# Output projection of a hybrid decoder step: the last columns' weights loaded over three column groups, the samples in two halves, two stores a token tile

## The chip, the cores and the metric

The kernel runs on one core of one Trainium2 chip, as one launch. The metric is the device time of that launch in microseconds. A core has five instruction streams that run side by side and wait for one another by semaphores: TensorE (PE in the profile, with PEld for its weight loads), VectorE (DVE), ScalarE (ACT), GpSimd (POOL) and SyncE (SP). Sixteen DMA engines move data; here SP's queue issues the weight loads and the stores of the results, and POOL's queue the loads of the residual rows.

## The reference

One decoder layer (RWKV-7 and HGRN2 branches side by side) on 256 prompt tokens and 64 sample tokens, width 2048, all in float32. The change touches only its last part:

```python
merged = sigmoid(p[..., OFF_GA:OFF_GB]) * (y_a @ proj_a) + sigmoid(p[..., OFF_GB:]) * (y_b @ proj_b)
y = x + merged @ w_out                                   # w_out: 2048 x 2048
y_prompt, y_sample = rms_norm(y, final_norm_g)           # over all 2048 columns of a token
```

The final norm of a token needs the sum of the squares of all its 2048 columns, so no column of a token can be stored before its last column is there.

## The kernel before

The input projection and the two branches (the lines up to 1376, put in order by a planner of the kernel's own) and the merge (lines 1400 to 1420) are not touched. What follows is the output projection with the final norm.

Every float32 operand is held as a high part and a low part (`fp32r`), and a product is made of three matmuls: high times high, low times high, high times low. The 320 tokens are three token tiles, `j` = 0 and 1 for 128 prompt tokens each and `j` = 2 for the 64 samples. For the samples the high and the low part stand side by side as 128 columns of one stationary operand (`ms`), so two matmuls do instead of three, and the two halves of the result's partitions are summed afterwards. The merged tokens are the stationary operand, the weights `w_out` the moving one, 512 columns at a time.

The 2048 columns of `w_out` are four column groups of 512, `n` = 0 to 3; the 2048 rows are 8 steps `kk` of 256 (two `k` of 128 each).

- `columns(n, kk, pool, tag)` (line 1440) loads one piece of 256 x 512 (512 KB): a DMA on SP's queue into `raw`, of which there are three buffers in turn for all pieces; a cast on ACT to `whi`; a subtraction on DVE to `wlo`. With an empty tag `whi` and `wlo` are a ring of three buffers each; with a tag they are tiles of their own in the pool `last`.
- `rows(pt, j, k, hi, lo)` (line 1450) issues the three (or two) matmuls of one `k` for one token tile.
- `add(pt, j, n)` (line 1462) adds the result in PSUM to the residual row in `yx[j]` (for the samples twice, once for each half of the partitions) and squares the 512 columns on ACT, with the sum into one column of `ssq`.

Groups 0 to 2 (from line 1475) run `kk` outermost: each step is 16 matmuls, for the three token tiles in turn, into three PSUM tiles. After a group, `add` is called for each token tile and the columns are multiplied by the gain `fg`. In group 2 each step also calls `columns(3, kk)`, so the last group's eight pieces are loaded beside group 2's own; seven of them have tiles of their own and the eighth takes its place in the ring.

The last columns (from line 1490) run the token tile outermost: all 48 matmuls of tile 0, then its `add`, its norm (`ssq` summed, Ln, Exp, which gives the scale `r`), its four scalings and four stores of 512 columns, while the matmuls of tile 1 run; the same for tile 1; and for the samples 32 matmuls with nothing behind them to cover their norm, scalings and stores.

What sets the order: in groups 0 to 2 PE's instructions stand in the order written, and ACT and DVE are put in order by the framework's scheduler. In the last columns PE, ACT and DVE all stand in the order written. SP issues its DMAs in the order written, each when its buffer is free. The residual rows `yx` and the gains `fg` are loaded by POOL's queue (lines 1429 and 1430) into memory that the input projection held until its last matmul.

Of the kernel before, what the change touches and what calls it, by code (L numbers as in the profile page):

```python
# [9 lines left out]
F32 = mybir.dt.float32  # L10
F32R = mybir.dt.float32r
U8 = mybir.dt.uint8
AF = mybir.ActivationFunctionType
ALU = mybir.AluOpType
# [8 lines left out]
KT = D // 128  # L23
# [249 lines left out]
def hybrid_step(ctx, tc, x_prompt, x_sample, state_rwkv, state_hgrn, state_shift, norm_g, w_in,  # L273
# [3 lines left out]
    nc = tc.nc  # L277
    V, S, G, T = nc.vector, nc.scalar, nc.gpsimd, nc.tensor

    S.add_instruction(mybir.InstLoadActFuncSet(  # L280
        name=nc.get_next_instruction_name(), act_func_set_id=EXP_LN_SET, ins=[], outs=[]))
# [4 lines left out]
    wpool = ctx.enter_context(tc.tile_pool(name="wpool", bufs=1))  # L286
# [67 lines left out]
    with tc.tile_pool(name="start", bufs=1) as st, \  # L354
# [9 lines left out]
        for hf in range(2):  # L364
            cs = slice(1024 * hf, 1024 * hf + 1024)
# [24 lines left out]
        for h in range(2):  # L390
            sl = slice(32 * h, 32 * h + 32)
            G.affine_select(out=sel[sl], in_=sel[sl], pattern=[[-1, 4], [0, 128]],
                            compare_op=ALU.not_equal, fill=1.0, base=0, channel_multiplier=1)
        rows = st.tile([128, 128], F32, name="rows")
        G.memset(rows, 0.0)

        def row_dma(r0, n, src):
# [77 lines left out]
        ssq = [st.tile([128, 2], F32, name=f"ssq{j}") for j in range(3)]  # L475
# [46 lines left out]
        with tc.manual_schedule(engines={mybir.EngineType.PE, mybir.EngineType.Activation, mybir.EngineType.DVE,  # L522
# [70 lines left out]
            for j in range(2):  # L593
                high(j, 3)
                low(j, 3)
            ps = pst.tile([128, 512], F32, name="cps", tag="t")
            T.transpose(ps[:, :128], rows, ident)
            V.tensor_copy(cols, ps[:, :106])
            ps = pst.tile([128, 512], F32, name="sps", tag="t")
# [766 lines left out]
    with tc.manual_schedule():  # L1366
# [3 lines left out]
        V, S, G, T, Y = (book.proxy(e) for e in ("V", "S", "G", "PE", "Y"))  # L1370
        record_all()
        V, S, G, T = real
# [52 lines left out]
    yx = [xa[:, 0], xa[:, 1], xb[:64, 0]]  # L1425
    fg = xb[:, 1]
# [7 lines left out]

    last = ctx.enter_context(tc.tile_pool(name="last", bufs=1))
    pso = ctx.enter_context(tc.tile_pool(name="pso", bufs=2, space=PSUM))
    ssq = last.tile([128, 3, 4], F32, name="ssq")
    rs = [last.tile([128, 1], F32, name=f"rs{j}") for j in range(3)]

    def columns(n, kk, pool, tag):  # L1440
        raw = wpool.tile([128, 2, 512], F32, name="raw", tag="raw", bufs=3)
        nc.sync.dma_start(raw, w_out[0, 256 * kk:256 * kk + 256, 512 * n:512 * n + 512]
                          .rearrange("(k p) c -> p k c", p=128))
        hi = pool.tile([128, 2, 512], F32R, name="whi", tag="whi" + tag, bufs=1 if tag else 3)
        lo = pool.tile([128, 2, 512], F32R, name="wlo", tag="wlo" + tag, bufs=1 if tag else 3)
        S.copy(hi, raw)  # L1446
        V.tensor_sub(lo, raw, hi.bitcast(F32))  # L1447
        return hi, lo

    def rows(pt, j, k, hi, lo):  # L1450
        first, end = k == 0, k == KT - 1
        if j < 2:
            h, l = (t_[:, k, 128 * j:128 * j + 128] for t_ in (mhi, mlo))
            T.matmul(pt, h, hi, start=first, stop=False)  # L1454
            T.matmul(pt, l, hi, start=False, stop=False)  # L1455
            T.matmul(pt, h, lo, start=False, stop=end)  # L1456
        else:
            h = ms[:, k].rearrange("p x t -> p (x t)")
            T.matmul(pt, h, hi, start=first, stop=False)
            T.matmul(pt, h, lo, start=False, stop=end)  # L1460

    def add(pt, j, n):
        y = yx[j][:, 512 * n:512 * n + 512]
        if j < 2:
            V.tensor_add(y, y, pt)
        else:
            for sl in HS:
                V.tensor_add(y, y, pt[sl])
        jk = last.tile([128, 512], F32, name="jk", tag="jk", bufs=2)
        m = y.shape[0]  # L1470
        S.activation(jk[:m], y, AF.Square, accum_out=ssq[:m, j, n:n + 1])

    out_tiles = lambda: [pso.tile([128, 512], F32, name=f"po{j}", tag=f"o{j}") for j in range(3)]
    tail = []
    with tc.manual_schedule(engines={mybir.EngineType.PE}):
        for n in range(3):
            pts = out_tiles()
            for kk in range(8):
                hi, lo = columns(n, kk, wpool, "")
                for q in range(2):  # L1480
                    for j in range(3):
                        rows(pts[j], j, 2 * kk + q, hi[:, q], lo[:, q])
                if n == 2:
                    tail.append(columns(3, kk, *((last, str(kk)) if kk < 7 else (wpool, ""))))
            for j in range(3):
                add(pts[j], j, n)
                y = yx[j][:, 512 * n:512 * n + 512]
                V.tensor_mul(y, y, fg[:y.shape[0], 512 * n:512 * n + 512])

    with tc.manual_schedule(engines={mybir.EngineType.PE, mybir.EngineType.Activation, mybir.EngineType.DVE}):  # L1490
        pts = out_tiles()
        for j in range(3):
            for k in range(KT):
                hi, lo = tail[k // 2]
                rows(pts[j], j, k, hi[:, k % 2], lo[:, k % 2])
            add(pts[j], j, 3)
            m = yx[j].shape[0]
            r = rs[j][:m]
            V.tensor_reduce(r, ssq[:m, j, :], axis=mybir.AxisListType.X, op=ALU.add)
            S.activation(r, r, AF.Ln, scale=1.0 / D, bias=eps_n[:m])  # L1500
            S.activation(r, r, AF.Exp, scale=-0.5)
            dst = y_prompt[0, 128 * j:128 * j + 128, :] if j < 2 else y_sample.rearrange("b l d -> (b l) d")
            for n in (0, 1, 3, 2):
                cs = slice(512 * n, 512 * n + 512)
                y = yx[j][:, cs]
                if n == 0 or n == 2:
                    V.tensor_scalar(y, y, r, 0.0, op0=ALU.mult, op1=ALU.add)
                elif n == 1:
                    S.activation(y, y, AF.Copy, scale=r)
                else:  # L1510
                    V.scalar_tensor_tensor(y, y, r, fg[:m, cs], op0=ALU.mult, op1=ALU.mult)
                nc.sync.dma_start(dst[:, cs], y)


# [26 lines left out]
```

## Time and profile before

| What | us |
|---|---|
| median of three timed runs | 1170.04 (1169.23 to 1171.2) |
| the profiled execution's own time | 1167.92 |
| its span, first to last instruction | 1166.2 |
| first matmul of group 0 | 1035.88 |
| first matmul of group 1, of group 2 | 1064.98, 1094.01 |
| first matmul of the last columns: tile 0, tile 1, samples | 1127.17, 1138.36, 1149.55 |
| last matmul ends | 1157.19 |
| scale of the samples ready | 1160.15 |

All of the trace's times are from the start of the span. In a row of the timeline stand the start and the length in us, the engine, the line, the operation and its operands (out<-in), and in brackets the idle time of the engine before it and what ended that. In a row of a group stand the count, the busy time in us and the mean length of one in ns. In a row of the busy time by stretch stand the stretch and its length, each engine's busy time and number of instructions, the granted clock of TensorE, the busy share of the DMA engines and GB/s. A row of waits has the total in us, the count and the longest.

### The profile page before, as it was taken

The page shows a single profiled execution, that of the slowest core. Times are in us where ns is not written, and L with a number is a line of the kernel's source. Part 1 is how long each engine was busy: PE and PEld are TensorE (multiplying, and loading weights), DVE is VectorE, ACT ScalarE, POOL GpSimd, SP SyncE. Part 2 cuts the span into 40 slices and gives each one's busy share as a digit, 9 for nine tenths or more (in the row PEclk, how much of TensorE's full clock was granted, in tenths as well). Part 3 has the DMA queues.
Part 4 walks back from the last instruction along what each step waited for, and adds up shares of the span by engine and source line. Part 5 has one row for each costly group of instructions (what it writes and reads, how often), then busy time and mean ns, then how long its engine had stood idle before and what let it go on. Part 6 is the DMA issues. An engine that isn't in the chain of part 4 may idle for free.

```text
span 1166.2 us, 20745 instructions
## 1 busy us (share of the span) xinstructions
PE 1140.5 (98%) x7791; PEld 1099.2 (94%) x7791; DVE 779.9 (67%) x1625; ACT 666.7 (57%) x1470; POOL 208.9 (18%) x429
## 2 busy tenths in 40 slices
PE   7899999999999999999999999999999999999996
PEld 6899999999999999999999999999999999988865
DVE  6878878878878778778779786444444444444542
ACT  6666766667667667666676667444444444433431
POOL 8532132222322321321421310000000000000000
PEclk9999999999999999999999999999999999999999
DMA  5734535434435435436335435555555555575532
GB/s 168 197 109 114 146 110 129 138 102 124 136 91 150 128 98 145 127 83 164 102 92 166 123 101 137 149 158 146 147 155 151 145 149 157 146 254 162 180 109 90
DMA packets 283833, 159.69 MB, mean 137 GB/s; under 512 B 22990, under 2 KB 273361, under 8 KB 283093
## 3 DMA queue, kind: packets, MB, share of 16 engines
q1 hardware_dynamic: 283220, 154.70, 47.1%
q0 software_dynamic: 512, 3.67, 1.0%
q8 instruction: 61, 1.00, 0.4%
q14 instruction: 40, 0.32, 0.1%
HBM read 148.53 MB, written 9.81 MB: 136 GB/s over the span
## 4 chain that ended last, share of the span: by engine, by line
PE 92%; DVE 3%; DMA 2%; ACT 1%; POOL 1%; issue 1%; DVEq 0%; SPq 0%; ACTq 0%; POOLq 0%
PE mps L1374 40%; PE a L1374 12%; PE mps L338 6%; PE mps L337 6%; PE mps L339 6%; PE b L1374 4%; DMA raw<-in_w_out_dram 2%; PE po L1456 2%; PE po L1454 2%; PE po L1455 2%; PE ppb L338 2%; PE ppa L338 2%; PE ppb L337 2%; PE ppa L337 2%; PE ppb L339 2%; PE ppa L339 2%
## 5 line engine op out<-in xcount | busy, mean ns | idle before, releaser
L1374 PE MATMUL mps<-hlo,whi 128*128 128x320 f32 x1088 | 344.7, 317 | 0.0
L1374 PE MATMUL mps<-hhi,whi 128*128 128x320 f32 x1088 | 344.1, 316 | 0.0
L1374 PE MATMUL mps<-hhi,wlo 128*128 128x320 f32 x1088 | 343.8, 316 | 0.0
L1374 PEld LDWEIGHTS mps<-hlo,whi 128*128 128x128 f32 x1088 | 204.9, 188 | 4.8 <-issue 4.5
L1374 PEld LDWEIGHTS mps<-hhi,whi 128*128 128x128 f32 x1088 | 204.9, 188 | 1.7 <-issue 1.4
L1374 PEld LDWEIGHTS mps<-hhi,wlo 128*128 128x128 f32 x1088 | 204.9, 188 | 0.2
L328 DVE TENSOR_TENSOR wlo<-raw,whi 128x1024 fp32r<-128x1024 f32 x88 | 107.8, 1225 | 125.3 <-ACT whi L327 125.1
L1374 ACT CAST whi<-raw 128x1024 fp32r<-128x1024 f32 x134 | 140.6, 1049 | 80.3 <-PE mps L1374 75.8
L327 ACT CAST whi<-raw 128x1024 fp32r<-128x1024 f32 x88 | 92.2, 1048 | 163.1 <-PE mps L338 104.8
L1374 DVE TENSOR_TENSOR wlo<-raw,whi 128x1024 fp32r<-128x1024 f32 x134 | 168.1, 1255 | 20.0 <-ACT whi L1374 19.4
L337 PE MATMUL mps<-hhi,whi 128*128 128x320 f32 x448 | 138.4, 309 | 0.0
L338 PE MATMUL mps<-hlo,whi 128*128 128x320 f32 x448 | 138.4, 309 | 0.0
L339 PE MATMUL mps<-hhi,wlo 128*128 128x320 f32 x448 | 138.4, 309 | 0.0
L337 PEld LDWEIGHTS mps<-hhi,whi 128*128 128x128 f32 x448 | 84.1, 188 | 0.0
L338 PEld LDWEIGHTS mps<-hlo,whi 128*128 128x128 f32 x448 | 84.1, 188 | 0.0
L339 PEld LDWEIGHTS mps<-hhi,wlo 128*128 128x128 f32 x448 | 84.1, 188 | 0.0
L1447 DVE TENSOR_TENSOR wlo<-raw,whi 128x1024 fp32r<-128x1024 f32 x32 | 39.0, 1224 | 46.4 <-ACT whi L1446 46.1
L1446 ACT CAST whi<-raw 128x1024 fp32r<-128x1024 f32 x32 | 33.6, 1051 | 56.8 <-DMA raw<-in_w_out_dram 26.9
L1429 POOL DMA_DIRECT2D xb<-in_x_sample_dram x1 | 0.7, 721 | 341.2 <-PE mps L339 341.2
L1454 PE MATMUL po<-whi,mhi 128*128 128x512 f32 x128 | 50.4, 393 | 1.7 <-ACT whi L1446 1.0
L1456 PE MATMUL po<-wlo,mhi 128*128 128x512 f32 x128 | 50.5, 394 | 1.3 <-DVE wlo L1447 1.3
L1455 PE MATMUL po<-whi,mlo 128*128 128x512 f32 x128 | 50.1, 391 | 0.0
(408 smaller groups left out, 2341.4 us busy)
## 6 DMA issues: line engine op xcount, KB each, us to landing
raw<-in_w_in_dram SPq DMA_DIRECT2D x194, 512.0 KB
raw<-in_w_out_dram SPq DMA_DIRECT2D x32, 512.0 KB
raw<-in_proj_a_dram SPq DMA_DIRECT2D x16, 512.0 KB
raw<-in_proj_b_dram SPq DMA_DIRECT2D x16, 512.0 KB
s<-in_state_hgrn_dram SPq DMA_DIRECT2D x8, 512.0 KB
out_dram<-s SPq DMA_DIRECT2D x8, 512.0 KB
s<-in_state_rwkv_dram SPq DMA_DIRECT2D x8, 256.0 KB
out_dram<-s SPq DMA_DIRECT2D x8, 256.0 KB
```

The source lines that it names most:

```text
L327: S.copy(hi[:, ks], raw[:, ks])
L328: sub.tensor_sub(lo[:, ks], raw[:, ks], hi[:, ks].bitcast(F32))
L337: T.matmul(dst, hi[:, q, :], xhi[:, k, :], start=(k == 0), stop=False)
L338: T.matmul(dst, hi[:, q, :], xlo[:, k, :], start=False, stop=False)
L339: T.matmul(dst, lo[:, q, :], xhi[:, k, :], start=False, stop=(k == nk - 1))
L1374: o.fn(*o.args, **o.kw)
L1429: G.dma_start(yx[j], src)
L1446: S.copy(hi, raw)
L1447: V.tensor_sub(lo, raw, hi.bitcast(F32))
L1454: T.matmul(pt, h, hi, start=first, stop=False)
L1455: T.matmul(pt, l, hi, start=False, stop=False)
L1456: T.matmul(pt, h, lo, start=False, stop=end)
```

## The change

The pieces of the last columns are no longer all loaded in group 2. After steps 1, 4 and 7 of each group the next piece is loaded until there are seven: indices 0 to 2 in group 0, 3 to 5 in group 1, 6 in group 2. The eighth is loaded at the head of the last columns.

The samples' last 512 columns are made in two halves of 256: 32 matmuls of 256 columns into one PSUM tile, their `add` into a fourth column of `ssq`, then 32 more into another PSUM tile and their `add` into a fifth.

The scalings of each token tile go to other engines in part (columns 1024 to 1535 from DVE to ACT) and the four stores of 512 columns become two of 1024.

```diff
-    ssq = last.tile([128, 3, 4], F32, name="ssq")
+    ssq = last.tile([128, 3, 5], F32, name="ssq")
...
     def rows(pt, j, k, hi, lo):
+        pt = pt[:, :hi.shape[-1]]
...
-    def add(pt, j, n):
-        y = yx[j][:, 512 * n:512 * n + 512]
+    def add(pt, j, n, c0, w=512):
+        y = yx[j][:, c0:c0 + w]
         if j < 2:
-            V.tensor_add(y, y, pt)
+            V.tensor_add(y, y, pt[:, :w])
         else:
             for sl in HS:
-                V.tensor_add(y, y, pt[sl])
+                V.tensor_add(y, y, pt[sl, :w])
         jk = last.tile([128, 512], F32, name="jk", tag="jk", bufs=2)
         m = y.shape[0]
-        S.activation(jk[:m], y, AF.Square, accum_out=ssq[:m, j, n:n + 1])
+        S.activation(jk[:m, :w], y, AF.Square, accum_out=ssq[:m, j, n:n + 1])
...
-                if n == 2:
-                    tail.append(columns(3, kk, *((last, str(kk)) if kk < 7 else (wpool, ""))))
+                if kk % 3 == 1 and len(tail) < 7:
+                    tail.append(columns(3, len(tail), last, str(len(tail))))
             for j in range(3):
-                add(pts[j], j, n)
+                add(pts[j], j, n, 512 * n)
...
+        tail.append(columns(3, 7, wpool, ""))
         pts = out_tiles()
         for j in range(3):
-            for k in range(KT):
-                hi, lo = tail[k // 2]
-                rows(pts[j], j, k, hi[:, k % 2], lo[:, k % 2])
-            add(pts[j], j, 3)
+            w = 512 if j < 2 else 256
+            for n, pt in enumerate((pts[j],) if j < 2 else (pts[j], pso.tile([128, 512], F32, name="po0", tag="o0"))):
+                cs = slice(w * n, w * n + w)
+                for k in range(KT):
+                    hi, lo = tail[k // 2]
+                    rows(pt, j, k, hi[:, k % 2, cs], lo[:, k % 2, cs])
+                add(pt, j, 3 + n, 1536 + w * n, w)
...
-            V.tensor_reduce(r, ssq[:m, j, :], axis=mybir.AxisListType.X, op=ALU.add)
+            V.tensor_reduce(r, ssq[:m, j, :4 + j // 2], axis=mybir.AxisListType.X, op=ALU.add)
...
-            for n in (0, 1, 3, 2):
-                cs = slice(512 * n, 512 * n + 512)
-                y = yx[j][:, cs]
-                if n == 0 or n == 2:
-                    V.tensor_scalar(y, y, r, 0.0, op0=ALU.mult, op1=ALU.add)
-                elif n == 1:
-                    S.activation(y, y, AF.Copy, scale=r)
-                else:
-                    V.scalar_tensor_tensor(y, y, r, fg[:m, cs], op0=ALU.mult, op1=ALU.mult)
-                nc.sync.dma_start(dst[:, cs], y)
+            y = [yx[j][:, 512 * n:512 * n + 512] for n in range(4)]
+            V.tensor_scalar(y[0], y[0], r, 0.0, op0=ALU.mult, op1=ALU.add)
+            S.activation(y[1], y[1], AF.Copy, scale=r)
+            nc.sync.dma_start(dst[:, :1024], yx[j][:, :1024])
+            V.scalar_tensor_tensor(y[3], y[3], r, fg[:m, 1536:], op0=ALU.mult, op1=ALU.mult)
+            S.activation(y[2], y[2], AF.Copy, scale=r)
+            nc.sync.dma_start(dst[:, 1024:], yx[j][:, 1024:])
```

## The prediction

> **What bounds the kernel now.** I read the page first, then the busy time by stretch over the output projection, then PE's own waits, then the timelines of SP, POOL, ACT, DVE and PE around those waits.
>
> ```profile
> span 1166.2 us, 20745 instructions
> ```
>
> The change touches only the last 130 us of this. Cut at the first matmul of each column group and, for the last columns, of each token tile:
>
> ```profile
> core 0: us, PE busy (x) PEld busy (x) DVE busy (x) ACT busy (x) POOL busy (x), PEclk, DMA share, GB/s
> 1035.88:1064.98 29.10, 29.10 (x128) 24.10 (x129) 11.49 (x13) 8.39 (x11) 0.00 (x0) 1.00 0.68 239
> 1064.98:1094.01 29.03, 29.03 (x130) 24.02 (x128) 14.96 (x16) 12.29 (x16) 0.00 (x0) 1.00 0.54 163
> 1094.01:1127.17 33.16, 30.81 (x130) 23.55 (x128) 20.38 (x22) 14.67 (x19) 0.00 (x0) 1.00 0.55 174
> 1127.17:1138.36 11.19, 11.19 (x49) 9.03 (x48) 3.60 (x6) 1.92 (x6) 0.00 (x0) 1.00 0.01 1
> 1138.36:1149.55 11.19, 11.19 (x49) 9.03 (x48) 2.39 (x5) 1.94 (x5) 0.00 (x0) 1.00 0.28 94
> 1149.55:1157.19 7.64, 7.63 (x33) 5.83 (x31) 2.39 (x5) 1.95 (x5) 0.00 (x0) 1.00 0.40 137
> 1157.19:1166.20 9.01, 0.00 (x0) 0.00 (x0) 3.06 (x6) 1.94 (x5) 0.00 (x0) 0.73 0.26 58
> ```
>
> PE is busy all through but in group 2 and behind the last matmul; so its waits, its matmuls and that last chain set the end. Groups 0 and 1 take 29.0 us for 128 matmuls, 0.227 us from start to start. Group 2 has the same matmuls and takes 33.16: **4.1 us are lost**, at full clock, to waits and to the slower restarts behind them. The last line is the chain behind the last matmul, 9.0 us. What PE waits for:
>
> ```profile
> PEld po L1456 <- DVE wlo L1447: 3.0, 4, 1.0
> PEld po L1454 <- ACT whi L1446: 1.9, 2, 1.2
> ```
>
> ```profile
> 1092.34 1.05 ACT L1446 CAST whi<-raw 128x1024 fp32r<-128x1024 f32 x1 [0.94 <-DMA raw<-in_w_out_dram]
> ...
> 1123.60 1.05 ACT L1446 CAST whi<-raw 128x1024 fp32r<-128x1024 f32 x1 [1.05 <-DMA raw<-in_w_out_dram]
> ```
>
> The weights are late. In group 2 sixteen loads, eight of its own and eight of the last columns, go through three `raw` buffers. From the first of these casts to the second there are twelve loads in 31.3 us, 2.6 us each, where sixteen in 29 us ask for 1.8.
>
> **Part 1: the loads move.** Group 2 keeps its own eight and one of the others, 3.2 us for each, more than the 2.6 that the ring took. So the waits of group 2 go: **-4.1 us**. The eighth load (index 7) goes to the head of the last columns. Its DMA is alone on SP's queue, but its cast and subtraction now stand behind group 2's squares on ACT and scalings on DVE, and the squares and sums of the last columns stand behind them. The last of the scalings before was:
>
> ```profile
> 1130.96 0.68 DVE L1488 TENSOR_TENSOR xb<-xb 64x512 f32<-64x512 f32 x1 [0.85 <-ACT jk L1471]
> ```
>
> It ends 4.5 us after the last columns began at 1127.17; with 1.05 and 1.23 us for cast and subtraction the weights are there at 6.8 us, and they are first used by matmul 42 of token tile 0, at 9.8 us. Cost nothing, with a cover of 3 us.
>
> Groups 0 and 1 get eleven loads each, four for every three steps (a step is 16 matmuls, 3.63 us): 2.7 us per load, against 2.6. That is tight, and in group 0 something else is on the DMA engines. `raw` has three buffers and SP issues in the written order, so the first extra load takes the third place and **each of group 0's loads from step 2 on moves one place back in the queue**. What the places are worth:
>
> ```profile
> 1028.33 0.72 POOL L1429 DMA_DIRECT2D xb<-in_x_sample_dram  x1 [341.16 <-PE mps L339]
> ```
>
> ```profile
> 1030.39 0.37 SPq L1442 DMA_DIRECT2D raw<-in_w_out_dram  x1
> ```
>
> ```profile
> 1033.00:1044.50 11.50, 10.82 (x54) 9.12 (x53) 3.48 (x6) 2.46 (x4) 0.00 (x0) 1.00 0.99 382
> ```
>
> ```profile
> 1035.10 1.05 ACT L1446 CAST whi<-raw 128x1024 fp32r<-128x1024 f32 x1 [2.47 <-PE ppb L338]
> ...
> 1043.64 1.05 ACT L1446 CAST whi<-raw 128x1024 fp32r<-128x1024 f32 x1 [6.79 <-DMA raw<-in_w_out_dram]
> 1045.53 1.05 ACT L1446 CAST whi<-raw 128x1024 fp32r<-128x1024 f32 x1 [0.84 <-DMA raw<-in_w_out_dram]
> ```
>
> ```profile
> 1044.72 1.23 DVE L1447 TENSOR_TENSOR wlo<-raw,whi 128x1024 fp32r<-128x1024 f32 x1 [6.85 <-ACT whi L1446]
> ```
>
> ```profile
> 1043.23 0.39 PE L1454 MATMUL po<-whi,mhi 128*128 128x512 f32 x1
> ```
>
> From 1028.33 on POOL's queue issues the loads of the residual rows and the gains, and from 1033 to 1044.5 the DMA engines are 0.99 busy. SP's third load landed ahead of that and was cast at 1035.10, when its weight buffer came free; the fourth (issued at 1030.39) sat in the crowd and was cast at 1043.64, ACT waiting for it. Before, the third was step 2's and the fourth step 3's, needed at 1043.23 + 3.63 = 1046.9. Now the fourth is step 2's, and step 2 starts at 1043.23 (the PE row is its first matmul). Nothing in the change starts this DMA earlier: it waits for step 0's subtraction to free the buffer, as before. So `whi` of step 2 is there at 1043.64 + 1.05 = 1044.69. `wlo` follows with a subtraction that began at 1044.72 and takes 1.23, 1045.95, and the third matmul, the first that reads it, starts at about 1046.0 instead of 1043.23 + 2 x 0.227 = 1043.7: 2.3 us late. A restart costs a bit more, as in group 2:
>
> ```profile
> 1118.85 0.50 PE L1456 MATMUL po<-wlo,mhi 128*128 128x512 f32 x1 [0.53 <-DVE wlo L1447]
> ```
>
> 0.50 instead of 0.39, so 0.1 for the restart on `whi` or `wlo`, and 0.1 for slower matmuls behind it, both in the 4.1 of group 2 too. **+2.5 us**. Step 3 then begins 2.5 us later, at 1049.3, and its load (the fifth, cast at 1045.53) is in time; from there each three steps bring four loads, and the wait just had gives 2.5 us of lead to live on. I take no further wait in groups 0 and 1. The extra casts and subtractions, 6 x 1.05 on ACT and 6 x 1.23 on DVE, lie in engines that are 29 to 52% busy there.
>
> Sum of part 1: -1.6 us at the start of the last columns.
>
> **Part 2: the samples in halves.** 32 matmuls of 512 columns become 64 of 256, each with its own weight load. No such stream is in the trace; the nearest rows:
>
> ```profile
> 1033.14 0.31 PE L339 MATMUL ppb<-ybh,wlo 128*128 128x320 f32 x1
> ...
> 1034.46 0.31 PE L339 MATMUL ppb<-ybh,wlo 128*128 128x320 f32 x1
> ```
>
> ```profile
> 1127.17 0.40 PE L1454 MATMUL po<-whi,mhi 128*128 128x512 f32 x1
> ...
> 1137.00 0.39 PE L1454 MATMUL po<-whi,mhi 128*128 128x512 f32 x1
> ```
>
> ```profile
> 97.39 0.36 PE L1374 MATMUL a<-fd,jr_sum 128*128 128x256 f32 x1
> 97.59 0.27 PE L1374 MATMUL a<-uv,bk 128*128 128x128 f32 x1
> ```
>
> Nine matmuls of 320 columns in 1.32 us are 0.147 each; 512 columns take 0.227. The line through both gives 0.120 for 256, the lower end. In the last columns a matmul of 512 takes 0.234 (42 from 1127.17 to 1137.00) where its weights lie in the tiles kept for them, and 0.227 (the 6 up to 1138.36) where they lie in the ring; half to all of these 0.007 gives 0.124 to 0.127. The upper end is the one 256-column matmul on split operands in the trace: 0.20, with a change of operand kind behind it. I take 0.124, by the streams, since they are the same operation and the 0.20 row pays for the change: 63 x 0.124 + 0.28 (the 0.39 of a row of 512 less 256 columns) = 8.1 against 7.64, **+0.5 us** (+0.2 to +5.3).
>
> The Trainium skill, "TensorE: Matmul & The Clock Gate", Part 3, The mechanism, speaks against the halves: a weight load overlaps a running matmul only when it goes to other rows of the array. These loads all take the full array, so by that rule each of the 32 added would stand on the path. The trace disagrees: loads of 0.19 us and matmuls of 320 columns share 0.147 us.
>
> What the halves buy is a shorter chain behind the last matmul:
>
> ```profile
> 1157.21 1.40 DVE L1468 TENSOR_TENSOR xb<-xb,po 64x512 f32<-64x512 f32 x2 [3.68 <-PE po L1460]
> ```
>
> ```profile
> L1374 DVE TENSOR_TENSOR rl<-y,yh 64x256 fp32r<-64x256 f32 x16 | 6.7, 422 | 2.2 <-ACT yh L1374 1.2 <-PE mps L1374 0.5
> ```
>
> ```profile
> L1374 ACT ACTIVATE w<-R 128x256 f32<-128x256 f32 x8 | 3.3, 409 | 0.0
> L1471 ACT ACTIVATE jk<-xb 64x512 f32<-64x512 f32 x4 | 2.5, 630 | 8.1 <-DVE xb L1468 7.8 <-ACT jk L1471 0.4
> ```
>
> Two sums of 0.42 instead of 1.40 together, -0.55; a square of 0.41 instead of 0.63, -0.2. **-0.8 us**. The first half's sums and square lie under the second half's matmuls. The sum over five columns instead of four costs nothing I can see.
>
> **Part 3: two stores a tile.** For tiles 0 and 1 this is under the matmuls of the next tile. For the samples:
>
> ```profile
> 1160.15 0.72 ACT L1509 ACTIVATE xb<-xb,rs 64x512 f32<-64x512 f32 x1
> ```
>
> ```profile
> 1160.66 0.50 SPq L1512 DMA_DIRECT2D out_dram<-xb  x1
> ```
>
> ```profile
> GB/s 0 0 0 0 0 0 0 0 0 0 140 234 187 164 234 211 199 176 234 211 199 199 222 211 152 24 0 0 0 0 0 0 0 0 0 0 0 0 0 0
> ```
>
> The GB/s row cuts 1160 to 1167 us into 40. The four stores, 0.52 MB, flow without a gap from 1161.75 to 1164.4 at some 200 GB/s, 1.1 us behind the first issue, and the span ends 1.8 us after the flow. So the first issue and the bytes set the end, not the number of issues. Now the first store needs the 0.72 us on ACT as well as the 0.48 on DVE: it is issued 0.24 us later. Same bytes, same rate: **+0.2 us**. If the larger pieces flowed at the 382 GB/s that the loads reached, the second store, which is ready about 1.45 us after the scale (two times 0.72 on ACT), would land 1.1 us sooner than now. Range -1.1 to +0.2; I take the row of the same 64 rows.
>
> **Sum.** -4.1 + 2.5 + 0.5 - 0.8 + 0.2 = **-1.7 us**: the span goes from 1166.2 to 1164.5, the profiled execution from 1167.9 to 1166.2. That execution lies 2.1 us under the median of the three timed runs, 1170.04 (1169.23 to 1171.2), so against those: **1168.3**.
>
> **The rivals.**
>
> *The load for step 2 is in time.* Then the +2.5 falls away: -4.2, 1165.8. For it: SP's order or a buffer freed earlier would do. Against it: the fourth issue at 1030.39 follows step 0's subtraction, which no edit touches, and the crowd on the DMA engines is POOL's.
>
> *The loads fall behind further.* Eleven loads at 2.6 us fill 28.7 of 29.0 us, and DVE's sums and scalings at a group's end hold up subtractions and with them `raw` buffers. If group 0 or 1 loses one more wait like the one at step 2: +0.8, 1170.8. Against it: part of the 2.6 in group 2 is those held-up buffers, and the weight ring of three steps carries lead over a group's end.
>
> *The halves cost two matmuls each.* If a 256-column matmul with its weight load takes the 0.20 us of the one row: 63 x 0.20 + 0.28 = 12.9 us against 7.64, +5.3 in place of +0.5, in sum +3.1: **1173.1, slower**. It decides from 0.15 us a matmul on, where 64 of them eat the rest of the gain. The rule of the Trainium skill named in part 2 points to this case. Against it: the streams of 320 and 512 columns, whose weight loads hide.
>
> **How the numbers follow.** My forecast 0.57, the load in time 0.22, further behind 0.12, the halves 0.09. Within 0.2% is 2.3 us, about what a measurement of this kernel can tell from no change. The forecast lies 0.6 us inside it, so of its 0.57 a quarter, 0.15, falls under faster, 0.41 under no change and 0.01 under slower; the load in time is faster (0.22); further behind is no change but for 0.02; the halves are slower. Faster 0.37, same 0.51, slower 0.12. The range: from the load in time with 0.3 of the stores' bound, 1165.5, to the further wait, 1170.9; the halves and half of what lies at the other end are left out.
>
> **What would show it.** Right: group 2 near 29.1 us, no waits of PE there; one wait at step 2 of group 0, on `whi` and then `wlo`, with ACT idle until a `raw` DMA near 1043.6; the samples' 64 matmuls at 0.12 to 0.13 us; two sums of 0.42 us behind the last matmul; two stores whose flow ends 4.4 us or more after the scale. Wrong: a group 0 of 29 us (then 1165.8); waits in group 1 or at matmul 42 of the last columns; matmuls of 256 columns above 0.15 us; a last store well above 200 GB/s.

## The result, and the profile after

The changed kernel takes 1175.51 us (median of six runs, 1174.87 to 1176.4) against 1169.88 for the kernel before (six runs, 1167.62 to 1171.2): **1.0048 times as long, 95% interval 1.0038 to 1.0059**. I had forecast 1168.3, with 1170.9 as the upper end. It is slower, some 5.6 us, where I had put 0.12 on slower.

The profiled execution took 1175.25 us. Busy time by stretch of the changed kernel, cut as before at the first matmul of each group, of the last columns, of the samples' last columns, and at the end of the last matmul (columns: stretch, length, busy time and count of PE, PEld, DVE, ACT, POOL, granted clock, DMA share, GB/s):

```profile
span 1173.6 us, 20807 instructions
...
1038.03:1070.63 32.60, 30.42 (x128) 23.71 (x129) 12.93 (x13) 10.76 (x12) 0.00 (x0) 1.00 0.69 236
1070.63:1102.74 32.11, 29.90 (x129) 23.73 (x128) 17.22 (x18) 13.11 (x17) 0.00 (x0) 1.00 0.57 179
1102.74:1135.02 32.28, 29.94 (x130) 23.79 (x128) 16.03 (x18) 11.42 (x16) 0.00 (x0) 1.00 0.38 120
1135.02:1157.40 22.38, 22.38 (x97) 18.07 (x96) 5.59 (x10) 4.47 (x12) 0.00 (x0) 1.00 0.12 48
1157.40:1165.17 7.77, 7.77 (x65) 7.55 (x63) 2.83 (x6) 3.07 (x8) 0.00 (x0) 1.00 0.34 135
1165.17:1173.56 8.39, 0.00 (x0) 0.00 (x0) 2.12 (x5) 2.34 (x6) 0.00 (x0) 0.80 0.30 63
```

The three groups take 32.6, 32.1 and 32.3 us in place of 29.1, 29.0 and 33.2: 96.99 in sum against 91.29, **+5.7**. Without waits a group takes 29.0, so 9.9 us are lost now, in every group, where 4.1 were lost, in group 2 alone. The samples' columns take 0.13 us more (7.77 against 7.64) and the chain behind them 0.62 less (8.39 against 9.01). From the first matmul of group 0 to the end that is +5.2 us. The other 2.2 of the difference between the two spans lie ahead of 1038.03, in code that the change doesn't touch. PE's and its weight loads' waits in the changed kernel (total, count, longest):

```profile
PE po L1457 <- DVE wlo L1447: 4.5, 6, 1.0
...
PE po L1455 <- ACT whi L1446: 2.2, 3, 1.0
```

```profile
PEld po L1457 <- DVE wlo L1447: 7.8, 8, 1.5
...
PEld po L1455 <- ACT whi L1446: 3.4, 3, 1.4
```

The timeline of PE in the changed kernel shows where they lie. These matmuls stand behind a wait, in groups 0, 1 and 2:

```profile
1046.55 0.50 PE L1455 MATMUL po<-whi,mhi 128*128 128x512 f32 x1 [1.02 <-ACT whi L1446]
...
1067.30 0.50 PE L1457 MATMUL po<-wlo,mhi 128*128 128x512 f32 x1 [0.60 <-DVE wlo L1447]
...
1074.99 0.50 PE L1455 MATMUL po<-whi,mhi 128*128 128x512 f32 x1 [0.57 <-ACT whi L1446]
...
1081.28 0.50 PE L1457 MATMUL po<-wlo,mhi 128*128 128x512 f32 x1 [0.92 <-DVE wlo L1447]
...
1107.12 0.50 PE L1455 MATMUL po<-whi,mhi 128*128 128x512 f32 x1 [0.59 <-ACT whi L1446]
...
1113.54 0.50 PE L1457 MATMUL po<-wlo,mhi 128*128 128x512 f32 x1 [1.04 <-DVE wlo L1447]
```

1046.55 is step 2 of group 0, the wait that I had forecast. The wait at step 7 of group 0 (1067.30) and the pairs of groups 1 and 2, at the heads of steps 1 and 2, I had not. ACT in the changed kernel, ahead of those waits:

```profile
1063.81 2.00 ACT L1446 CAST whi<-raw 128x1024 fp32r<-128x1024 f32 x2 [3.44 <-DMA raw<-in_w_out_dram]
...
1072.94 1.99 ACT L1446 CAST whi<-raw 128x1024 fp32r<-128x1024 f32 x2 [5.23 <-DMA raw<-in_w_out_dram]
...
1095.94 2.96 ACT L1446 CAST whi<-raw 128x1024 fp32r<-128x1024 f32 x3 [5.19 <-DMA raw<-in_w_out_dram]
...
1105.08 1.99 ACT L1446 CAST whi<-raw 128x1024 fp32r<-128x1024 f32 x2 [6.18 <-DMA raw<-in_w_out_dram]
```

Four times ACT is idle for 3.4 to 6.2 us for a transfer and then makes two or three casts without a break: the second's data was there already. The order of the loads on SP and of the casts on ACT says why. This is the order in the built program (0.7 is the piece of group 0, step 7; x2 is the piece of index 2 of the last columns):

```
SP   ... 0.5 0.6 0.7 x2  1.0 1.1 x3  1.2 ... 1.6 1.7 x5  2.0 2.1 x6  2.2
ACT  ... 0.5 0.6 x2  0.7 1.0 x3  1.1 1.2 ... 1.6 x5  1.7 2.0 x6  2.1 2.2
```

DVE's subtractions stand as ACT's casts do. Only PE's order is written out by hand in the groups; on ACT and DVE the framework chose, and put four extra pieces (x2, x3, x5, x6) ahead of a step's piece that SP loads before them. So the cast of the step's piece, whose data has landed, stands behind a cast that waits for the next transfer, and the step's raw buffer stays taken, which delays the loads after. That is **theory A**. **Theory B**: the loads are simply too many for three raw buffers (one load every 2.7 us). **Theory C**, for group 0: the first extra piece's target is memory that the merge ahead still uses, so it holds its raw buffer until then. ACT in the changed kernel:

```profile
1045.46 1.04 ACT L1446 CAST whi<-raw 128x1024 fp32r<-128x1024 f32 x1 [10.68 <-DMA raw<-in_w_out_dram]
...
1046.71 0.24 ACT L1418 CAST ms<-mt 128x64 fp32r<-128x64 f32 x1
1048.26 2.00 ACT L1446 CAST whi<-raw 128x1024 fp32r<-128x1024 f32 x2 [1.31 <-DVE ms L1419]
```

1045.46 is step 2's cast. The first extra piece, third in SP's order, is cast at 1048.26 only, released by the merge's last operation on DVE (`ms`, L1419), which needs ACT's cast at 1046.71, and that stands behind step 2's cast. In the kernel before it stands behind step 2's cast too, but that was made at 1035.10, and `ms` followed soon:

```profile
1036.60 0.24 ACT L1418 CAST ms<-mt 128x64 fp32r<-128x64 f32 x1
```

So the extra piece delays step 2's load, and with it the release of the memory that it waits for itself.

### The profile page after: what moved, and what is told of

The parts are those of the page before. It is cut to its first block, busy times and chain, and to the rows that moved or that the text cites. A ratio compares the mean times of both kernels' runs of the same rounds, so it can differ in the third digit from the quotient of the medians.

```text
span 1173.6 us, 20807 instructions
## 1 busy us (share of the span) xinstructions
PE 1144.0 (97%) x7823; PEld 1102.6 (94%) x7823; DVE 778.1 (66%) x1624; ACT 668.2 (57%) x1475; POOL 209.5 (18%) x429
## 4 chain that ended last, share of the span: by engine, by line
PE 91%; DMA 3%; DVE 3%; ACT 1%; issue 1%; POOL 1%; ACTq 0%; SPq 0%; DVEq 0%; POOLq 0%
PE mps L1374 40%; PE a L1374 12%; PE mps L338 6%; PE mps L337 6%; PE mps L339 6%; PE b L1374 4%; DMA raw<-in_w_out_dram 2%; PE po L1457 2%; PE po L1455 2%; PE po L1456 2%; PE ppb L338 2%; PE ppa L338 2%; PE ppb L337 1%; PE ppa L337 1%; PE ppa L339 1%; PE ppb L339 1%
```

## The experiments

Each ratio is to the kernel before, on the same chip, with its 95% interval.

| Run | Median us | Ratio | Groups 0, 1, 2 in us |
|---|---|---|---|
| loads alone | 1176.34 | 1.0051 (1.0033 to 1.0069) | 33.8, 32.0, 31.9 |
| in order | 1170.14 | 0.9993 (0.9981 to 1.0004) | 31.9, 30.6, 29.0 |
| halves alone | 1169.62 | 0.9988 (0.9973 to 1.0002) | 29.1, 29.0, 31.7 |
| stores alone | 1170.93 | 1.0005 (0.9994 to 1.0016) | 29.1, 29.0, 31.8 |
| in order, later places | 1166.08 | 0.9967 (0.9956 to 0.9978) | 29.1, 29.0, 29.0 |
| and a raw buffer of their own | 1166.25 | 0.9974 (0.9961 to 0.9986) | 29.1, 29.0, 29.0 |
| weights 32 bytes on | 1169.92 | 1.0001 (0.9991 to 1.0011) | 29.1, 29.0, 31.9 |
| combined | 1165.91 | 0.9964 (0.9950 to 0.9979) | 29.1, 29.0, 29.0 |
| later places, free order | 1167.38 | 0.9978 (0.9966 to 0.9990) | 29.7, 29.8, 29.0 |
| in order, first piece moved | 1167.57 | 0.9974 (0.9964 to 0.9985) | 29.2, 30.6, 29.0 |

**Loads alone.** The kernel before with

```diff
-                if n == 2:
-                    tail.append(columns(3, kk, *((last, str(kk)) if kk < 7 else (wpool, ""))))
+                if kk % 3 == 1 and len(tail) < 7:
+                    tail.append(columns(3, len(tail), last, str(len(tail))))
...
+        tail.append(columns(3, 7, wpool, ""))
```

> The kernel before with the new places of the last columns' loads alone: whole samples' columns and four stores a token tile as before. The theory that the loads cost everything: groups 0 to 2 of the projection take about 97.0 us as in the changed kernel against 91.3 before, and the end keeps the 9.0 us of before, so some 5 to 6 us slower than before. The rival, that the halves and stores also lose time or disturb the loads: groups 0 to 2 nearer 91.3 us than 97.0 and the time within 2 us of before.

The three groups take 97.7 us, the end takes 9.0, and the ratio is that of the whole change. So the loss is all in part 1, and neither the halves nor the stores disturb it.

**In order.** The changed kernel with the extra pieces' casts and subtractions held behind those of the piece loaded before them:

```diff
+    made = []
+    inst = lambda x: getattr(x, "ins", x)
...
-        S.copy(hi, raw)
-        V.tensor_sub(lo, raw, hi.bitcast(F32))
+        with ExitStack() as behind:
+            if n == 3 and kk < 7:
+                for x in made[-1]:
+                    behind.enter_context(tc.issue_after(x))
+            made.append((inst(S.copy(hi, raw)), inst(V.tensor_sub(lo, raw, hi.bitcast(F32)))))
```

> The changed kernel, with the cast and the subtraction of each extra piece kept behind those of the step's piece that was loaded before it, on ScalarE and on VectorE. Theory A (the four pieces that stand in the written order behind an extra one on ACT wait for a transfer that comes later): the waits of groups 1 and 2 (3.1 and 3.3 us) shrink to under 1 us each and step 7 of group 0 loses its 1.0 us, the waits of group 0 at step 2 stay (2.3 us); groups 0 to 2 near 90 us, some 5 us faster than the changed kernel, at or below the time before. Theory B (three raw buffers at some 2.7 us a load don't bring eleven pieces in a group's time): groups 1 and 2 still lose 2 to 3 us each, the time within 1.5 us of the changed kernel.

Groups 0, 1 and 2 by stretch, in the in-order kernel:

```profile
1035.94:1067.85 31.91, 30.30 (x129) 23.79 (x129) 13.11 (x14) 11.89 (x13) 0.00 (x0) 1.00 0.72 246
1067.85:1098.43 30.58, 29.31 (x129) 23.95 (x128) 18.70 (x19) 13.98 (x18) 0.00 (x0) 1.00 0.62 196
1098.43:1127.45 29.02, 29.02 (x130) 24.02 (x128) 14.93 (x17) 9.82 (x15) 0.00 (x0) 1.00 0.39 123
```

With the same loads at the same places group 2 loses nothing, group 1 loses 1.6 us instead of 3.1, and the whole stands 0.55% under the changed kernel by the two ratios, 6.4 us. Theory A holds for groups 1 and 2; B, which wanted 2 to 3 us in each, falls. Two things stayed: 2.9 us in group 0, where A had 2.3, and the 1.6 us in group 1, where it had under 1. By the starts of PE's matmuls group 0's loss lies at step 2 (1.9 us), step 3 (0.3) and step 5 (0.6).

**Halves alone and stores alone.** The two other parts, each on the kernel before.

> The kernel before with the samples' last columns in two halves alone. My working: 64 matmuls of 256 columns take 0.1 to 0.5 us more than the 32 whole ones, the add and square behind the last one take 0.8 us less; groups 0 to 2 unchanged (33.2 us in group 2); 0.3 to 0.7 us faster. The rival that two halves cost two matmuls each: samples' last columns 5 us longer and the kernel slower.

> The kernel before with two stores a token tile alone. My working: the first store waits for ScalarE's scaling (0.7 us behind the row scale in place of 0.5), so from the row scale to the last store's landing it is 0.2 us longer, and everything ahead is as before: 0 to 0.3 us slower, not to be told from no change by the timing. The rival: fewer packets on the queue let the last store land earlier, 0.3 us faster or more.

The samples' columns and the end behind them in the kernel with the halves alone:

```profile
1150.62:1158.38 7.76, 7.76 (x65) 7.55 (x63) 3.22 (x7) 2.46 (x7) 0.00 (x0) 1.00 0.40 135
1158.38:1166.66 8.28, 0.00 (x1) 0.00 (x0) 2.52 (x6) 1.73 (x5) 0.00 (x0) 0.63 0.29 63
```

and the end in the kernel with two stores alone:

```profile
1159.53:1168.65 9.12, 0.00 (x0) 0.00 (x0) 2.65 (x5) 2.55 (x6) 0.00 (x0) 0.69 0.27 58
```

The halves cost 0.12 us of matmuls (7.76 against 7.64) and save 0.73 at the end: 0.6 us in favour. The stores cost 0.11. Neither ratio is clear of 1; the sizes come from the stretches. Both of my rivals fall: that two halves cost two matmuls each, and that fewer stores land earlier.

**In order, and later places.** All extra pieces go later: two, two and three of them in the three groups, where the change had three, three and one. Group 0 gets its first behind step 4:

```diff
-                if kk % 3 == 1 and len(tail) < 7:
+                if 8 * n + kk in (4, 7, 10, 13, 16, 19, 22):
```

> The kernel with the extra pieces kept in order on ScalarE and VectorE, and all extra pieces later: behind steps 4 and 7 of group 0, 2 and 5 of group 1, 0, 3 and 6 of group 2, so that none stands ahead of group 0's steps 2 to 4. Theory C (the first extra piece holds one of three raw buffers from 1030 to 1049 us, since its target memory is free only after the merge, and the step's loads issued behind it come late): group 0 loses under 0.5 us where the in-order kernel lost 2.9; with at most 1.6 us left in group 1, some 3 us less than the in-order kernel, 0.25% faster than before or more. Against it (three raw buffers at this rate are too few in group 0 wherever the extra piece stands): group 0 still loses 2 us or more at a later step and the time stays within 1 us of the in-order kernel.

No wait is left. The same three groups:

```profile
1039.02:1068.15 29.13, 29.13 (x128) 24.11 (x129) 13.90 (x15) 10.49 (x13) 0.00 (x0) 1.00 0.75 270
1068.15:1097.17 29.02, 29.02 (x130) 24.03 (x128) 17.58 (x19) 13.19 (x18) 0.00 (x0) 1.00 0.65 202
1097.17:1126.18 29.01, 29.01 (x129) 24.03 (x128) 15.21 (x17) 11.23 (x16) 0.00 (x0) 1.00 0.40 128
```

It is the change as described, with halves and two stores, and 0.33% faster than the kernel before: the idea of the change was sound, its order and its places were not. All places moved here, and groups 0 and 1 have ten loads each in place of eleven, so it doesn't say alone what counted.

**In order, first piece moved.** The first extra piece goes from behind step 1 to behind step 4. The second, which the change put there, goes to behind step 5, so two pieces move, not one; the other five stand as the change put them, and groups 0 and 1 keep their eleven loads.

```diff
-                if kk % 3 == 1 and len(tail) < 7:
+                if 8 * n + kk in (4, 5, 7, 9, 12, 15, 17):
```

> The in-order kernel with the first extra piece alone at another place, behind step 4 of group 0 in place of step 1; the other six stand where the change put them. If it is that piece and its raw buffer, held until the merge frees the target's memory, that costs group 0 its 2.9 us: the waits at steps 2 and 3 go, and 0 to 1 us is left there. For group 1's step 2 (1.6 us, whose subtraction stands behind VectorE's three adds) two ways: it goes as well, if its loads were late only since group 0 began late, or it stays at 1 to 1.7 us. If neither moves, the rate of eleven pieces in a group's time is what costs.

```profile
1038.02:1067.17 29.15, 29.15 (x128) 24.10 (x129) 12.68 (x13) 10.78 (x13) 0.00 (x0) 1.00 0.77 269
1067.17:1097.74 30.57, 29.41 (x129) 23.87 (x128) 19.16 (x20) 14.65 (x19) 0.00 (x0) 1.00 0.64 201
```

Of group 0's 2.9 us 0.1 is left. What stood at steps 2 and 3 (2.1 us) was the first piece's, since the second is loaded behind step 4's piece in both kernels; the 0.6 at step 5, behind which the second piece now stands, may be either's. Eleven loads are not too many for group 0's time. That the first piece's raw buffer was held by the merge's memory is read from the ACT rows above, and not tried apart from its place in the queue. Group 1 keeps its 1.6, all at the head of step 2. DVE in this kernel, from the subtraction of group 1's step 1 on; that of x3 (1069.53) stands behind it:

```profile
1067.76 1.23 DVE L1453 TENSOR_TENSOR wlo<-raw,whi 128x1024 fp32r<-128x1024 f32 x1 [0.23 <-ACT whi L1453]
1069.53 1.23 DVE L1453 TENSOR_TENSOR wlo<-raw,whi 128x1024 fp32r<-128x1024 f32 x1 [0.55 <-ACT whi L1453]
1070.67 1.28 DVE L1472 TENSOR_TENSOR xa<-xa,po 128x512 f32<-128x512 f32 x2
...
1075.02 1.21 DVE L1453 TENSOR_TENSOR wlo<-raw,whi 128x1024 fp32r<-128x1024 f32 x1
```

and DVE in the kernel in order with later places:

```profile
1067.22 1.37 DVE L1472 TENSOR_TENSOR xa<-xa,po 128x512 f32<-128x512 f32 x2
...
1071.02 1.22 DVE L1453 TENSOR_TENSOR wlo<-raw,whi 128x1024 fp32r<-128x1024 f32 x1
```

In the first, group 0 ends at 1067.17. The sums at its end stand behind x3's subtraction and begin at 1070.67, 3.5 us behind the group's end; step 2's subtraction stands behind them, at 1075.02. PE in the same kernel:

```profile
1076.29 0.50 PE L1463 MATMUL po<-wlo,mhi 128*128 128x512 f32 x1 [1.16 <-DVE wlo L1453]
```

In the second no extra piece stands between step 1 and the sums. They begin at 1067.22, in a group that ends at 1068.15, and step 2's subtraction begins at 1071.02, in time. The subtraction of step 1 ahead of x3's ends at 1068.99 (1067.76 and 1.23), so without x3 the sums could have begun 1.7 us earlier. I read from this that a piece ahead of the sums costs group 1 its 1.6 us; that piece alone was not moved.

**Later places, free order.** The later places without the order being held.

> The changed kernel with the extra pieces at the later places (behind steps 4 and 7 of group 0, 2 and 5 of group 1, 0, 3 and 6 of group 2), and the casts and subtractions left in the order that they get of themselves: on ScalarE five extra pieces still stand ahead of a step's piece that was loaded before them. If the order (A) costs by itself wherever the extra pieces stand: 1 to 3 us of waits on the steps' whi and wlo come back in groups 0 to 2, the time 1 us or more above the run with order and later places together. If the order only costs where the loads are late already: no waits and the time of that run, 0.3% below before.

All seven extra pieces on ACT, and six on DVE, stand ahead of a step's piece that was loaded before them; I had counted five. PE's waits in this kernel:

```profile
PE po L1457 <- DVE wlo L1447: 0.8, 2, 0.5
...
PEld po L1457 <- DVE wlo L1447: 1.6, 2, 0.9
```

Two waits, 0.6 us in group 0 and 0.8 in group 1: 1.4 us, and the median is 1.3 over that of the ordered run (measured on another chip, each against the kernel before there; the two intervals overlap). By the waits the wrong order costs by itself, but far less than where the places are bad too: places alone recover most of the loss.

**A raw buffer of their own.** As the ordered run with later places, and

```diff
-        raw = wpool.tile([128, 2, 512], F32, name="raw", tag="raw", bufs=3)
+        raw = (last if tag else wpool).tile([128, 2, 512], F32, name="raw", tag="rawt" if tag else "raw", bufs=1 if tag else 3)
```

> As the run with the first extra piece later, and the seven extra pieces load through one raw buffer of their own. Theory B's remainder (what is still lost is for want of raw buffers): the waits of groups 0 to 2 go from 1 to 2 us to under 0.5 us, 1 us faster than that run. If what is left comes from VectorE's three adds and scalings at the end of a group, which stand ahead of the subtraction for step 2 of groups 1 and 2: the same waits at that step as in that run, and the time within 0.5 us of it.

There was no wait left to take away, and nothing was gained (the intervals overlap). Three raw buffers are enough at these places.

**The weights 32 bytes on.** Aimed at the 0.234 us of a matmul in the last columns against 0.227 in the groups; the kernel before with

```diff
+    last.tile([128, 8], F32, name="pad")
```

> The kernel before with one unused tile of 32 bytes a partition ahead in the memory that the last columns' weights lie in, so that they start 32 bytes later, at the same place modulo 64 as the ring of the steps' weights. If the 0.234 us of a 512-column matmul in the last columns against 0.227 in the groups comes from the place: 0.227 in the last columns, 3.63 us for 16 in place of 3.74, 128 of them 0.8 us less. If it comes from something else: 3.74 us as before and no difference.

Tiles 0 and 1 take 22.36 us instead of 22.38 and the kernel no less: the place isn't it. The cause of the 0.007 us stays open. (For the halves the place does count a little, as the next run shows.)

**Combined.** Halves, four stores, pieces in order at the places below, and the 32 bytes.

```diff
...
-                if kk % 3 == 1 and len(tail) < 7:
+                if 8 * n + kk in (5, 7, 11, 13, 15, 19, 21):
...
```

> The halves, four stores a token tile as before, the extra pieces in order behind steps 5 and 7 of group 0, 3, 5 and 7 of group 1, 3 and 5 of group 2, and the 32 bytes ahead. From the runs so far: group 2's 4.1 us of waits gone, the halves 0.6 us, the place 0.8 us if it counts, together 4.7 to 5.5 us less than before (0.40 to 0.47%), if no new wait comes in groups 0 and 1; each wait at a step 2 behind VectorE's adds would take 1 to 1.6 us of it back.

0.36% faster than before, no waits, and not to be told from the ordered run with later places. From the first matmul of group 0 to the end its stretches add up to 125.41 us, against 130.32 in the profiled execution of before: the 4.9 us that I expected. The medians of the timed runs differ by 3.7 only, the ratio makes it 4.2, and its interval (2.5 to 5.8) does not exclude the 4.9. Group 2 of three kernels that load as the kernel before does speaks for the smaller figure; these are the kernels with halves alone, with stores alone, and with the 32 bytes:

```profile
1096.55:1128.23 31.68, 30.14 (x130) 23.59 (x128) 20.18 (x21) 14.67 (x18) 0.00 (x0) 1.00 0.57 182
```

```profile
1097.70:1129.52 31.82, 30.29 (x130) 23.61 (x128) 20.18 (x22) 14.84 (x19) 0.00 (x0) 1.00 0.57 182
```

```profile
1096.99:1128.89 31.90, 30.52 (x130) 23.62 (x128) 20.36 (x22) 14.58 (x19) 0.00 (x0) 1.00 0.57 181
```

They lose 2.7 to 2.9 us there, not the 4.1 of the one execution profiled before the change. So the waits to be won were more likely some 2.8 us, and 2.8 plus the halves' 0.6 is near what the medians show. The samples' columns of the combined kernel have something else:

```profile
1149.00:1156.60 7.60, 7.59 (x65) 7.39 (x63) 3.22 (x7) 2.46 (x7) 0.00 (x0) 1.00 0.41 138
```

The 64 matmuls of 256 columns take 7.60 us with the 32 bytes, where they take 7.76 or 7.77 in the profiles of all seven other kernels with halves. That is 0.16 us for the place of the weights; no run has the halves and the 32 bytes alone.

## Why the prediction was wrong, point by point

- **"I take no further wait in groups 0 and 1."** This is the step that failed: the three groups took 5.7 us more than in the execution before, where the sum had 1.6 less. After the wait at step 2, group 0 lost another 1 us, most of it at step 7, and group 1 lost 3.1. I had compared rates, 2.7 us a load against the ring's 2.6, and the rate was not what cost: in the kernels in order eleven loads pass group 0 with 0.1 us lost (first piece moved) and eleven pass group 2 with none (later places). What cost was the order on ACT and DVE together with the places: of the 9.9 us lost, 4.5 are left when the order is held at the same places, none when the places are later too, and 1.4 when only the places are later. I took it that casts follow the loads, though only PE's order is written out in the groups; the order of those engines decides which transfer a landed piece waits behind.
- **"So the waits of group 2 go: -4.1 us."** Two faults. Group 2 did lose its own waits, but got 3.3 us of others, at steps 1 and 2, from the extra pieces that stand ahead of the casts of 1.7 and of 2.1. In order they are gone, so that much of the term was right. And its size came from one execution: where three others lose 2.7 to 2.9, I should have taken 4.1 as the upper bound.
- **The wait at step 2 of group 0, +2.5 us.** Right in place and nearly in size: step 2's cast, the fourth load, came 7.4 us behind the group's first matmul (1045.46 - 1038.03; I had 7.8), behind 10.68 us of idle time on a DMA, then `whi` and `wlo` in turn, 2.1 us for both and 0.3 more at step 3. "Step 3 ... in time" was slightly off. Moving that piece removes it, so the cause was right: step 2's load lost its place in SP's queue to the extra piece. I had not seen how long the extra piece then holds its raw buffer.
- **The rival "the loads fall behind further"** was the nearest, and named the sums at a group's end as one of its causes; that is the 1.6 us in group 1 of the two ordered kernels. I priced it at one more wait of 2.5 us, which made the whole change +0.8. The three groups lost 9.9 us where I had 2.5 in the forecast and 5 in this rival. The bounds were too narrow: the same ring had lost 4.1 us in a group once, so one such loss in each group was the upper end to take, and I took one wait more in one.
- **Halves, +0.5 and -0.8.** Right in sign; +0.13 and, with the stores, -0.62 measured. A matmul of 256 columns starts every 0.119 us: the lower end of my range, the line through the rows of 320 and 512, was the better price.
- **The eighth piece at the head of the last columns, nothing.** Right: tiles 0 and 1 take 22.38 us, as before (twice 11.19).
- **Two stores, +0.2.** Right in sign, and 0.11 us in size. The first is issued 0.75 us behind the scale (1168.15 - 1167.40), as worked out. The end chain of the changed kernel:

```profile
1165.21 0.87 DVE L1469 TENSOR_TENSOR xb<-xb,po 64x256 f32<-64x256 f32 x2 [2.93 <-PE po L1461]
1166.11 0.42 ACT L1472 ACTIVATE jk<-xb 64x256 f32<-64x256 f32 x1 [3.29 <-DVE xb L1469]
...
1167.40 0.72 ACT L1511 ACTIVATE xb<-xb,rs 64x512 f32<-64x512 f32 x1
...
1168.15 0.50 SPq L1512 DMA_DIRECT2D out_dram<-xb  x1
1168.76 0.53 SPq L1515 DMA_DIRECT2D out_dram<-xb  x1
```

Two sums in 0.87 and a square in 0.42, as priced.

- **The base.** I set the sum against an execution that lies 2.1 us under the median and carried the difference over as constant. That execution began group 0 at 1035.88; of the others here with the same code ahead, one began at 1035.94 and the rest at 1038.0 to 1039.6. Its loss in group 2 was the largest of the four executions that load as before. The three groups of the other three take 89.8 to 90.0 us, so against those the changed kernel lost 7.0 to 7.2 us in its groups, not 5.7; that the 5.7 of the two profiles lies so near the 5.6 of the medians is luck.

## What to carry to other kernels

When a load is moved, follow it on every engine that handles it, and find out who sets the order there: a cast that waits for a later transfer, ahead of one whose data has landed, makes the earlier one late and holds its buffer. An idle stretch on a DMA with two casts back to back behind it is a mark of that in a timeline. Put a prefetch behind the loads that are needed first, and not ahead of the sums of a group's end. That the memory it goes to should be free already is read from the rows here, not tried by itself. A wait read from one execution may differ in the next: 4.1 us in one, 2.7 to 2.9 in three.

## What the runs showed that I had not expected

Matmuls can start closer together than their weight loads last. The prediction had seen it at 320 columns (0.147 us against 0.19); at 256 columns it goes on. In the samples' halves of the changed kernel (weight loads and matmuls in turn):

```profile
1164.65 0.28 PE L1461 MATMUL po<-wlo,ms 128*128 128x256 f32 x1
1164.66 0.19 PEld L1460 LDWEIGHTS po<-whi,ms 128*128 128x128 f32 x1
1164.77 0.28 PE L1460 MATMUL po<-whi,ms 128*128 128x256 f32 x1
1164.78 0.19 PEld L1461 LDWEIGHTS po<-wlo,ms 128*128 128x128 f32 x1
```

A matmul of 256 columns starts every 0.12 us, each with its own weight load of 0.19 us, and the records of the loads overlap each other. The rule of the Trainium skill that I had weighed ("TensorE: Matmul & The Clock Gate", Part 3, The mechanism: a weight load overlaps a running matmul only in other rows of the array) does not hold for this stream: all the loads take the full array, and 64 matmuls took 7.77 us. The same section also names a load into the background weight buffer as one that runs ahead of matmuls; no run here shows whether that is what happens.

A change of 0.6 us at the end, or of 0.1, is visible in the stretches of a profile and lost in the timed runs, where the interval reaches 1 to 2 us to either side.
